# Attention scores of two pairs of heads in one go, with turns for the third PSUM pool

## The chip, the cores and the metric

The kernel runs on one core of a Trainium2 chip. The metric is the device time of one execution in microseconds (us). Before the change three timed runs gave 740.46, 740.71 and 740.96 us, with a median of 740.71. TensorE multiplies matrices into PSUM, VectorE (DVE) and ScalarE (ACT) do elementwise work, SyncE (SP) issues the loads. Each engine works through its own instructions in order.

## The reference

Two layers of a decoder trunk on 256 tokens of width 1024, in float32. The first half of a layer projects x once to the q, k and v of two attention branches of 8 heads of 64 each, and to two gates:

```python
def hybrid_mixer(x, w_in, w_branch_sb, w_branch_moba, w_out):
    S = x.shape[1]
    proj = x @ w_in
...
    o_sb = stick_breaking_attention(heads(q_sb, SB_HEADS), heads(k_sb, SB_HEADS), heads(v_sb, SB_HEADS))
    o_mb = moba_attention(partial_rope(heads(q_mb, MOBA_HEADS), pos),
                          partial_rope(heads(k_mb, MOBA_HEADS), pos),
                          heads(v_mb, MOBA_HEADS))
    branch_sb = merge_heads(o_sb) @ w_branch_sb
    branch_mb = merge_heads(o_mb) @ w_branch_moba
    merged = jax.nn.sigmoid(g_sb) * branch_sb + jax.nn.sigmoid(g_mb) * branch_mb
    return merged @ w_out
```

The stick-breaking weights of a query are sigmoid(z) times the product of sigmoid(-z) over all later keys before the query. The MoBA branch is, with 256 tokens and blocks of 256, a causal softmax. After the mixer come a normalised residual, a gated feed-forward of width 2816, and a second normalised residual.

## The kernel before

**Products.** Every float32 operand is split in two: `hi` holds its value rounded for TensorE's faster float32 mode, `lo` what is left. A product is then three matmuls, hi with hi, hi with lo and lo with hi. ScalarE makes hi (the cast at L48), VectorE makes lo (the subtraction at L53). The helper lines L48, L53 and L344 (`mm`) stand for most of the work, so the profile is read by tile names.

**Weights.** The weights come in 122 granules a layer of 128 x 1024 floats (512 KB) in the order in which they are used. `WeightStream` loads each to one of NRAW raw buffers, ScalarE and VectorE split it into one of ten places of the rings `whi` and `wlo`, and the raw buffer is free again. A projection to feature rows (`feat_major`: q and k of a stick-breaking pair, gates) uses a granule in 24 matmuls of 256 columns, one to token rows (`both_tokens`: v, and q and k of MoBA) in 12 of 512 columns.

**Attention.** Heads go in pairs: two heads of 64 rows lie in the 128 rows of a tile. The scores of a pair (`scores`, L460) are 12 matmuls on 64 rows each, two at a time, one for either head: three products for the first 128 queries against 128 keys, and three for the others against 256. VectorE adds the mask. In a stick-breaking pair (`sb_line`) ScalarE then computes two sigmoids, `keep` and `beta`, VectorE scans `keep` to `inc` and multiplies it into `beta`. In a MoBA pair (`mb_line`) VectorE takes maxima, ScalarE exponentials with their sums, VectorE scales. Then, for both (`weighted`): six transposes (L357) to `pT`, a split, six matmuls with v to `o`, and another split to the branch's output.

**Order.** The order of all instructions is written out when the program is built. The projections are the main line. Everything else is a generator, a "side", that yields the time at which its next step may be put in. The class `Weave` keeps an estimated time `t` of TensorE and of the other engines from the costs of what has been issued, and `tick`, called after every three matmuls, steps the sides that are due. The estimates set the order alone; the chip waits by semaphores.

**PSUM.** Three pools of two buffers each: `psM` for the projections (one bank a buffer), `psC` for the transposes of q, k, x and the feed-forward, and for `o` (one bank), `psB` for scores and `pT` (two banks). In layer order the stick-breaking pairs 0 to 3 are projected between the k and v of MoBA and the first gate; the MoBA pairs follow while gates 1 to 7 are projected, one every MB_GAP of estimated time.

Of the kernel before, what the change touches and what calls it, by code (L numbers as in the profile page):

```python
# [7 lines left out]
F32 = mybir.dt.float32  # L8
# [6 lines left out]
P = 128  # L15
# [19 lines left out]
class Weave:  # L35
# [31 lines left out]
    def _step(self, side):  # L67
        self.busy = True
        try:
            side[1] = next(side[0])  # L70
        except StopIteration:
            self.sides.remove(side)
        self.busy = False

    def tick(self):
# [104 lines left out]
ORDER = {2 * i + j: 4 * j + i for i in range(4) for j in range(2)}  # L180
NRAW = 6
NSPLIT = 10
# [15 lines left out]
def hybrid_trunk_kernel(ctx: ExitStack, tc: tile.TileContext, w, xT_in, x_in, ln_in,  # L198
# [32 lines left out]
    def bankB(name, shape):  # L231
        return psB.tile(shape, F32, tag="B", name=name)

    weave = Weave()
    rings = [p.tile([P, NSPLIT * GCOLS + on], F32R, name=n)
             for p, n, on in ((ring0, "whi", ON[0]), (ring1, "wlo", ON[1]))]
# [11 lines left out]
    xT_lo = big.tile([P, KC, S], F32R, name="xT_lo")  # L248
    mask = page2.tile([P, 2, P], F32, name="mask")
    warm = small.tile([P, 1], F32, tag="nmu", name="warm")  # L250
# [47 lines left out]
    nc.scalar.activation(warm, zero, AF.Sigmoid)  # L298
    busy = bankC("busy", [P, 512])
    for i in range(N_WARM):  # L300
        nc.tensor.matmul(busy, idle[:, :P], idle, start=True, stop=True)
# [61 lines left out]
    def pe_done():  # L363
        return weave.t + HOP
# [63 lines left out]
    def rope_line(name, ps, t, put):  # L428

        tmp = work.tile([P, 8, DH], F32, tag="T", name=f"{name}_tok{t}")  # L430
# [3 lines left out]
        a, b = (p.tile([P, n], F32, tag=tag, name=f"{name}_{tag}{t}")[:, :8 * ROPE]  # L434
                .rearrange("p (h r) -> p h r", h=8) for p, tag, n in ((page1, "ra", 240), (page2, "rb", 208)))
# [15 lines left out]
        yield from put(tp, slice(t * P, (t + 1) * P), pe_done())  # L451

    def scores(s, q, k, m):

        for c0, qs, ks in ((0, slice(0, P), slice(0, P)), (P, slice(P, S), slice(0, S))):
            for a, b in ((0, 0), (0, 1), (1, 0)):
                for h, rows in enumerate(ROWS):
                    nc.tensor.matmul(s[:, h, c0:c0 + ks.stop], q[a][rows, qs], k[b][rows, ks],  # L460
                                     start=a == b, stop=a == 1)
                weave.t += 0.11
        e = pe_done()
        yield e
        diag = s.rearrange("p h (a c) -> p h a c", c=256)[:, :, :, :P]
        e = dve(e, 512, nc.vector.tensor_add, diag, diag,
                mask[:, m, None, None, :].to_broadcast([P, 2, 2, P]))
        yield e
        return e

    def weighted(name, p, wt, v, oT, e):

        yield e + MARGIN
        pT = bankB(f"{name}_pT", [P, 2, 512])
        p_hi = page0.tile([P, 2, 384], F32R, tag="ph", name=f"{name}_ph")
        p_lo = page1.tile([P, 2, 384], F32R, tag="pl", name=f"{name}_pl")
        pe_after(e)
# [4 lines left out]
        e = pe_done()  # L482
        yield e
        e = yield from split_line(p_hi, p_lo, pT[:, :, :384], 768, e)
        yield e + MARGIN
        o = bankC(f"{name}_o", [P, 2, S])
        vs = slice(p * P, (p + 1) * P)
        pe_after(e)
        for part, a, b, first, last in ((o, 0, slice(0, S), True, False),
# [3 lines left out]
            mm(part, v[0][:, a, vs], p_lo[:, :, b], False, last)  # L493
        e = pe_done()
        yield e
        for h, hs in enumerate(ROWS):
            e = act(e, S, nc.scalar.copy, oT[0][hs, p, :], o[hs, h, :])
        yield e
        for h, hs in enumerate(ROWS):
            dve(e, S, nc.vector.tensor_sub, oT[1][hs, p, :], o[hs, h, :], oT[0][hs, p, :].bitcast(F32))  # L500

    BLOCKS = [(h, i, a, b) for h in range(2) for i, (a, b) in enumerate(((0, P), (P, 384)))]

    def sb_line(name, p, ps, hi, lo, v, oT, done):
        e = yield from split_line(hi, lo, ps, 512, pe_done())
        yield e + MARGIN
        s = bankB(f"{name}_s", [P, 2, 512])
        pe_after(e)
        e = yield from scores(s, *(((hi[:, i, :], lo[:, i, :])) for i in range(2)), 0)
        keep = work.tile([P, 2, 384], F32, tag="T", name=f"{name}_keep")  # L510
        beta = work.tile([P, 2, 384], F32, tag="T", name=f"{name}_beta")
        e1 = act(e, 768, nc.scalar.activation, keep, s[:, :, :384], AF.Sigmoid, scale=-0.125)
        e2 = act(e, 768, nc.scalar.activation, beta, s[:, :, :384], AF.Sigmoid, scale=0.125)
        done.append(name)
        yield e1
        inc = work.tile([P, 2, 384], F32, tag="T", name=f"{name}_inc")
# [3 lines left out]
        e = dve(e2, 768, nc.vector.tensor_mul, beta[:, :, :383], beta[:, :, :383], inc[:, :, 1:])  # L520
        yield from weighted(name, p, beta, v, oT, e)

    def mb_line(name, p, q, k, v, oT, before, done):
        while len(before) < NPAIR:
            yield weave.t + 0.1
        yield weave.t + MB_GAP * p
        s = bankB(f"{name}_s", [P, 2, 512])
        e = yield from scores(s, q, k, 1)
        nmax = small.tile([P, 2, 2], F32, tag="nmax", name=f"{name}_nmax")
# [16 lines left out]
        yield from weighted(name, p, ex, v, oT, e)  # L546

    halves = [slice(h * 512, (h + 1) * 512) for h in range(2)]
# [15 lines left out]
    def norm_line(name, t, junk, gb):  # L564
# [14 lines left out]
        for h in range(2):  # L579
            yield ends[h] + MARGIN  # L580
            tp = bankC(f"{name}_tp{t}{h}", [P, 4, P])
# [6 lines left out]
            yield e  # L588
            xT_ready[t] = yield from split_line(xT_hi[:, ks, ts], xT_lo[:, ks, ts], tp, 512, e)

# [32 lines left out]
    for l in range(DEPTH):  # L623
# [37 lines left out]
        sides, sigmoids, exps, gates, waiting = [], [], [], [], []  # L661

        def sb_pair(p, g):
# [5 lines left out]
            sides.append(weave.start(sb_line(f"{L}sb{p}", p, ps, hi, lo, v_sb, o_sb, sigmoids)))  # L669

# [12 lines left out]

        sb_pair(0, G + 8)
        k_mb = pair_tiles(L + "kmb", [P, NPAIR, S])
# [12 lines left out]
        o_mb = pair_tiles(L + "omb", [P, NPAIR, S])  # L698
        for p in range(NPAIR):
            q, k = ([part[:, p, :] for part in t] for t in (q_mb, k_mb))  # L700
            sides.append(weave.add(mb_line(f"{L}mb{p}", p, q, k, v_mb, o_mb, sigmoids, exps)))
        for c in range(1, KC):
# [44 lines left out]
        def h_line(name, ps, j, t):  # L747
# [4 lines left out]
            e = dve(e, 256, nc.vector.tensor_mul, sg, sg, ps[:, 256:])  # L752
            yield e + MARGIN
            tp = bankC(name + "T", [P, 2, P])
# [5 lines left out]
            yield e  # L760
            yield from split_line(h_t[0][0][:, 2 * j:2 * j + 2, ts], h_t[0][1][:, 2 * j:2 * j + 2, ts], tp, 256, e)

# [138 lines left out]
```

## Time and profile before

| | us |
|---|---|
| median of three timed runs | 740.71 |
| the profiled execution | 740.71 |
| its span, from the first to the last instruction | 738.9 |
| TensorE busy | 729.4 |
| VectorE busy | 515.7 |
| ScalarE busy | 387.9 |

The profile is of one execution. In names of tiles `l0` and `l1` are the layers; `pqk`, `pk`, `pu`, `pg` and `pb` the projections of a stick-breaking q and k, MoBA's k, MoBA's v, a gate and the branches; `sb` and `mb` the two kinds of pair. Buffer numbers are left out, so four pairs share a name. Matmuls are pipelined: a row's duration is longer than the distance to the next row's start. A row with x2 or x6 holds that many instructions.

### The profile page before, as it was taken

The page shows a single profiled execution, that of the slowest core. Times are in us where ns is not written, and L with a number is a line of the kernel's source. Part 1 is how long each engine was busy: PE and PEld are TensorE (multiplying, and loading weights), DVE is VectorE, ACT ScalarE, POOL GpSimd, SP SyncE. Part 2 cuts the span into 40 slices and gives each one's busy share as a digit, 9 for nine tenths or more (in the row PEclk, how much of TensorE's full clock was granted, in tenths as well). Part 3 has the DMA queues.
Part 4 walks back from the last instruction along what each step waited for, and adds up shares of the span by engine and source line. Part 5 has one row for each costly group of instructions (what it writes and reads, how often), then busy time and mean ns, then how long its engine had stood idle before and what let it go on. Part 6 is the DMA issues. An engine that isn't in the chain of part 4 may idle for free.

```text
span 738.9 us, 12698 instructions
## 1 busy us (share of the span) xinstructions
PE 729.4 (99%) x5112; PEld 669.3 (91%) x5112; DVE 515.7 (70%) x742; ACT 387.9 (52%) x575; POOL 13.4 (2%) x20
## 2 busy tenths in 40 slices
PE   9999999999999999999999999999999999999996
PEld 7888999998799999988888899999987999999885
DVE  5998876696886676643687787667878866665416
ACT  5765665863565455532375565566546655544300
POOL 0000000000000000000000000000010000000001
PEclk9999999999999999999999999999999999999998
DMA  8867622474486555465256364126646855553501
GB/s 303 335 211 246 227 81 92 170 243 150 178 274 216 197 199 193 179 259 195 74 198 241 143 200 144 58 86 228 232 167 201 281 191 194 190 200 129 214 1 57
DMA packets 39994, 136.32 MB, mean 184 GB/s; under 512 B 4480, under 2 KB 6528, under 8 KB 39936
## 3 DMA queue, kind: packets, MB, share of 16 engines
q1 hardware_dynamic: 39792, 135.25, 52.2%
q8 instruction: 40, 0.66, 0.3%
q10 hardware_dynamic: 144, 0.26, 0.1%
q14 instruction: 18, 0.15, 0.1%
HBM read 134.45 MB, written 1.05 MB: 183 GB/s over the span
## 4 chain that ended last, share of the span: by engine, by line
PE 94%; DVE 3%; issue 1%; ACT 1%; POOL 1%; POOLq 0%; DVEq 0%; ACTq 0%
PE l1pf L344 13%; PE l0pf L344 13%; PE l0pd L344 8%; PE l0pg L344 6%; PE l1pg L344 6%; PE l1pe L344 4%; PE l1pd L344 4%; PE l0pqk L344 3%; PE l1pvq L344 3%; PE l1pb L344 3%; PE l0pb L344 3%; PE l1pqk L344 3%; PE l0pw L344 2%; PE l1pw L344 2%; PE l1pft L344 2%; PE l0pft L344 2%
## 5 line engine op out<-in xcount | busy, mean ns | idle before, releaser
L53 DVE TENSOR_TENSOR wlo<-raw,whi 128x1024 fp32r<-128x1024 f32 (+1 forms) x248 | 296.3, 1206 | 84.2 <-ACT whi L48 81.0
L48 ACT CAST whi<-raw 128x1024 fp32r<-128x1024 f32 (+1 forms) x247 | 253.6, 1037 | 84.8 <-PE l0pd L344 20.8
L344 PE MATMUL l1pf<-xT_hi,whi 128*128 128x256 f32 x288 | 79.7, 277 | 0.0
L344 PE MATMUL l1pf<-xT_hi,wlo 128*128 128x256 f32 x288 | 79.6, 276 | 0.0
L344 PE MATMUL l1pf<-xT_lo,whi 128*128 128x256 f32 x288 | 79.6, 276 | 0.0
L344 PE MATMUL l0pf<-xT_hi,whi 128*128 128x256 f32 x288 | 79.6, 276 | 0.0
L344 PE MATMUL l0pf<-xT_hi,wlo 128*128 128x256 f32 x288 | 79.5, 276 | 0.0
L344 PE MATMUL l0pf<-xT_lo,whi 128*128 128x256 f32 x288 | 79.5, 276 | 0.0
L344 PEld LDWEIGHTS l1pf<-xT_lo,whi 128*128 128x128 f32 x288 | 54.1, 188 | 0.0
L344 PEld LDWEIGHTS l1pf<-xT_hi,whi 128*128 128x128 f32 x288 | 54.1, 188 | 0.0
L344 PEld LDWEIGHTS l1pf<-xT_hi,wlo 128*128 128x128 f32 x288 | 54.1, 188 | 0.0
L344 PEld LDWEIGHTS l0pf<-xT_lo,whi 128*128 128x128 f32 x288 | 54.1, 188 | 0.0
L344 PEld LDWEIGHTS l0pf<-xT_hi,whi 128*128 128x128 f32 x288 | 54.1, 188 | 0.0
L344 PEld LDWEIGHTS l0pf<-xT_hi,wlo 128*128 128x128 f32 x288 | 54.1, 188 | 0.0
L344 PE MATMUL l1pg<-xT_hi,whi 128*128 128x256 f32 x128 | 36.6, 286 | 0.0
L344 PE MATMUL l0pg<-xT_hi,whi 128*128 128x256 f32 x128 | 36.6, 286 | 0.0
L344 PE MATMUL l1pg<-xT_hi,wlo 128*128 128x256 f32 x128 | 35.6, 278 | 0.0
L344 PE MATMUL l0pg<-xT_hi,wlo 128*128 128x256 f32 x128 | 35.6, 278 | 0.0
L344 PE MATMUL l1pg<-xT_lo,whi 128*128 128x256 f32 x128 | 35.5, 277 | 0.0
L344 PE MATMUL l0pg<-xT_lo,whi 128*128 128x256 f32 x128 | 35.5, 277 | 0.0
L344 PE MATMUL l0pd<-whi,l0h_hi 128*128 128x512 f32 x88 | 34.4, 391 | 0.0
L344 PE MATMUL l0pd<-whi,l0h_lo 128*128 128x512 f32 x88 | 34.3, 389 | 0.0
(382 smaller groups left out, 1764.0 us busy)
## 6 DMA issues: line engine op xcount, KB each, us to landing
raw<-in_w_dram SPq DMA_DIRECT2D x240, 512.0 KB, 4.1
ln<-in_ln_dram SPq DMA_DIRECT2D x8, 512.0 KB, 6.2
raw<-in_w_dram SPq DMA_DIRECT2D x7, 256.0 KB, 5.1
x<-in_x_dram SPq DMA_DIRECT2D x2, 512.0 KB, 6.7
out_dram<-x SPq DMA_DIRECT2D x3, 256.0 KB, 2.0
xT_raw<-in_xT_dram SPq DMA_DIRECT2D x4, 128.0 KB, 4.0
xT_raw<-in_xT_dram SPq DMA_DIRECT2D x2, 256.0 KB, 6.4
raw<-in_w_dram ACTq DMA_DIRECT2D x1, 256.0 KB, 2.8
```

The costliest lines, as they stand in the source:

```text
L48: f(*args, **kw)
L53: f(*args, **kw)
L344: nc.tensor.matmul(o, a, b, start=start, stop=stop)
```

## The change

The q and k of two stick-breaking pairs are projected next to each other (pairs 0 and 1, then MoBA's k and v, then pairs 2 and 3, then gate 0), and the granules are renumbered to match. `two_pairs` takes both buffers of `psB`, issues the scores of both pairs, 24 matmuls, and starts a side for each. The MoBA pairs go by two in the same way. `weighted` uses one tile `pp` for both split weights of all pairs; lists (`begun`, `turned`, `summed`, `passed`) keep the sides in an order in which a buffer is asked for after its last reader has been issued. The odd stick-breaking pair's `keep` gets a tile of its own, and its `beta` waits for the even pair's product. A step that takes a buffer of `psC` asks `turn` for the estimated time at which the buffer two turns earlier is left. Sides may yield nothing, which means "look again soon", and `finish` steps the next side that can go on. To make room there are five raw buffers in place of six; the rope's copies go to the pool of 4 KB units, and the mask to another page.

```diff
     def finish(self, sides):
-        left = [s for s in sides if s in self.sides]
-        while left:
-            side = min(left, key=lambda s: s[1])
-            self._step(side)
-            left = [s for s in left if s in self.sides]
+        while left := [s for s in sides if s in self.sides]:
+            for side in sorted(left, key=lambda s: s[1]):
+                if not self._step(side):
+                    break
...
 ORDER = {2 * i + j: 4 * j + i for i in range(4) for j in range(2)}
-NRAW = 6
+
+for _g in (0, NG_LAYER):
...
+        ORDER[_g + _i] = _g + _j
+NRAW = 5
...
+    def turn(e):
+
+        was = None
+        while True:
+            k = taken[0] - 2
+            if k >= 0 and k not in left:
+                yield
+            elif (e := max(e, left.get(k, 0.0))) == was:
+                break
+            else:
+                was = e
+                yield e + MARGIN
+        taken[0] += 1
+        return taken[0] - 1
...
+    def scores(pairs):
+
+
+        for s, q, k in pairs:
+            for c0, qs, ks in ((0, slice(0, P), slice(0, P)), (P, slice(P, S), slice(0, S))):
+                for a, b in ((0, 0), (0, 1), (1, 0)):
+                    for h, rows in enumerate(ROWS):
+                        nc.tensor.matmul(s[:, h, c0:c0 + ks.stop], q[a][rows, qs], k[b][rows, ks],
+                                         start=a == b, stop=a == 1)
+                    weave.t += 0.11
+        return pe_done()
...
-        p_hi = page0.tile([P, 2, 384], F32R, tag="ph", name=f"{name}_ph")
-        p_lo = page1.tile([P, 2, 384], F32R, tag="pl", name=f"{name}_pl")
+        begun.append(name)
+        mine = len(begun)
+        p_hi, p_lo = (pp[:, i] for i in range(2))
...
+        while len(summed) < mine:
+            yield
+        e = max(e, summed[-1])
+        yield e
         e = yield from split_line(p_hi, p_lo, pT[:, :, :384], 768, e)
-        yield e + MARGIN
+        turned.append(e)
+        i = yield from turn(e)
         o = bankC(f"{name}_o", [P, 2, S])
...
+    def two_pairs(line, name, ps, qks, free, e, sides, *args):
+
+
+        while len(turned) < free:
+            yield
+        e = max(e, *turned[max(free - 2, 0):free], 0.0)
+        yield e + MARGIN
+        ss = [bankB(f"{name}{p}_s", [P, 2, 512]) for p in ps]
+        pe_after(e)
+        e = scores([(s, *qk) for s, qk in zip(ss, qks)])
+        for p, s in zip(ps, ss):
+            sides.append(weave.add(line(f"{name}{p}", p, s, e, *args)))
...
-        both_tokens(f"{L}pk", G + 10, lambda t, ps: ropes.append(weave.start(rope_line(L + "kmb", ps, t, put_kmb))))
-        sb_pair(1, G + 14)
+        both_tokens(f"{L}pk", G + 12, lambda t, ps: ropes.append(weave.start(rope_line(L + "kmb", ps, t, put_kmb))))
...
         sb_pair(2, G + 20)
-        gate(0, G + 22)
-        sb_pair(3, G + 24)
+        sb_pair(3, G + 22)
+        gate(0, G + 24)
```

What this does to the order is shown at three places. A number behind a name is the buffer's in the program.

TensorE, in layer 0 at the scores of the third stick-breaking pair, before:

```order
L344 MATMUL l0pg_816<-xT_hi,wlo 128x256
L460 MATMUL l0sb_s<-l0qkhi_739 128x128 x2
L460 MATMUL l0sb_s<-l0qklo_740,l0qkhi_739 128x128 x2
L460 MATMUL l0sb_s<-l0qkhi_739,l0qklo_740 128x128 x2
L460 MATMUL l0sb_s<-l0qkhi_739 128x256 x2
L460 MATMUL l0sb_s<-l0qklo_740,l0qkhi_739 128x256 x2
L460 MATMUL l0sb_s<-l0qkhi_739,l0qklo_740 128x256 x2
L344 MATMUL l0pg_816<-xT_hi,whi 128x256
```

and now, where the fourth pair's stand right behind them (a gate product follows):

```order
L484 MATMUL l0sb_s<-l0qkhi_741 128x128 x2
L484 MATMUL l0sb_s<-l0qklo_742,l0qkhi_741 128x128 x2
L484 MATMUL l0sb_s<-l0qkhi_741,l0qklo_742 128x128 x2
L484 MATMUL l0sb_s<-l0qkhi_741 128x256 x2
L484 MATMUL l0sb_s<-l0qklo_742,l0qkhi_741 128x256 x2
L484 MATMUL l0sb_s<-l0qkhi_741,l0qklo_742 128x256 x2
L484 MATMUL l0sb_s<-l0qkhi_810 128x128 x2
L484 MATMUL l0sb_s<-l0qklo_811,l0qkhi_810 128x128 x2
L484 MATMUL l0sb_s<-l0qkhi_810,l0qklo_811 128x128 x2
L484 MATMUL l0sb_s<-l0qkhi_810 128x256 x2
L484 MATMUL l0sb_s<-l0qklo_811,l0qkhi_810 128x256 x2
L484 MATMUL l0sb_s<-l0qkhi_810,l0qklo_811 128x256 x2
```

The score products of a pair are the same twelve; in place of two visits between ordinary products there is one.

VectorE at the same pair, from the split of its q and k to its product, before (`wlo` is the lo part of a weight granule):

```order
L53 TENSOR_TENSOR l0qklo_740<-l0pqk_741,l0qkhi_739 128x512
L53 TENSOR_TENSOR wlo<-raw_666,whi 128x1024
L53 TENSOR_TENSOR wlo<-raw_705,whi 128x1024
L53 TENSOR_TENSOR l0sb_s<-l0sb_s,mask 128x4x128
L53 TENSOR_TENSOR wlo<-raw_728,whi 128x1024
L53 SCALAR_TENSOR_TENSOR l0sb_inc<-l0sb_keep,zero 128x128
L53 SCALAR_TENSOR_TENSOR l0sb_inc<-l0sb_keep,zero 128x256
L53 SCALAR_TENSOR_TENSOR l0sb_inc<-l0sb_keep,zero 128x128
L53 SCALAR_TENSOR_TENSOR l0sb_inc<-l0sb_keep,zero 128x256
L53 TENSOR_TENSOR l0sb_beta<-l0sb_beta,l0sb_inc 128x2x383
```

and now, from the last weight split ahead of both masks to the second pair's product:

```order
L53 TENSOR_TENSOR wlo<-raw_791,whi 128x1024
L53 TENSOR_TENSOR l0sb_s<-l0sb_s,mask 128x4x128 x2
L53 SCALAR_TENSOR_TENSOR l0sb_inc<-l0sb_keep,zero 128x128
L53 SCALAR_TENSOR_TENSOR l0sb_inc<-l0sb_keep,zero 128x256
L53 SCALAR_TENSOR_TENSOR l0sb_inc<-l0sb_keep,zero 128x128
L53 SCALAR_TENSOR_TENSOR l0sb_inc<-l0sb_keep,zero 128x256
L53 TENSOR_TENSOR l0sb_beta<-l0sb_beta,l0sb_inc 128x2x383
L53 SCALAR_TENSOR_TENSOR l0sb_inc<-l0sb_keep,zero 128x128
L53 SCALAR_TENSOR_TENSOR l0sb_inc<-l0sb_keep,zero 128x256
L53 SCALAR_TENSOR_TENSOR l0sb_inc<-l0sb_keep,zero 128x128
L53 SCALAR_TENSOR_TENSOR l0sb_inc<-l0sb_keep,zero 128x256
L53 TENSOR_TENSOR l0sb_beta<-l0sb_beta,l0sb_inc 128x2x383
```

Both masks stand ahead of the first pair's scans, and no weight split stands between the two pairs' work.

ScalarE at the end of layer 0's attention, from the cast of the last pair's transposes to its output, before:

```order
L48 CAST l0mb_ph<-l0mb_pT 128x768
L48 CAST whi<-raw_1168 128x1024
L48 ACT_TABLE_LOAD
L48 ACTIVATE l0gate_1474<-l0pg_1475 128x512
L48 CAST whi<-raw_1232 128x1024
L48 CAST l0omb_hi<-l0mb_o 64x256 x2
```

and now, from the third pair's transposes to the fourth pair's output:

```order
L48 CAST pp<-l0mb_pT 128x768
L48 ACT_TABLE_LOAD
L48 ACTIVATE l0gate_1452<-l0pg_1453 128x512
L48 CAST whi<-raw_1291 128x1024
L48 CAST whi<-raw_1305 128x1024
L48 CAST l0omb_hi<-l0mb_o 64x256 x2
L48 CAST pp<-l0mb_pT 128x768
L48 CAST whi<-raw_1344 128x1024
L48 ACTIVATE l0gate_1452<-l0pg_1528 128x512
L48 CAST l0omb_hi<-l0mb_o 64x256 x2
```

The last pair's cast stands behind the third pair's two output casts, since `pp` is one tile.

## Rows read from the trace of the kernel before

**Rows 1.** The page: its head, the busy time of the engines, and the shares of the engines in the chain of work that ended last.

```profile
span 738.9 us, 12698 instructions
...
PE 729.4 (99%) x5112; PEld 669.3 (91%) x5112; DVE 515.7 (70%) x742; ACT 387.9 (52%) x575; POOL 13.4 (2%) x20
...
PE 94%; DVE 3%; issue 1%; ACT 1%; POOL 1%; POOLq 0%; DVEq 0%; ACTq 0%
```

**Rows 2.** The list of waits, of TensorE alone: who waited for whom, us in total, times, longest us.

```profile
PE busy L301 <- DVE mhalf L297: 1.5, 1, 1.5
PE l1a_tp L357 <- DVE xT_lo L53: 0.4, 1, 0.4
PE l0a_tp L357 <- DVE xT_lo L53: 0.3, 1, 0.3
```

**Rows 3.** The timeline of TensorE around the scores of the third pair in layer 0, between gate products of 256 columns: start us, us, engine, line, operation, output and operands, rows and columns of the stationary side, moving operand, count.

```profile
75.34 0.28 PE L344 MATMUL l0pg<-xT_hi,whi 128*128 128x256 f32 x1
...
75.90 0.28 PE L344 MATMUL l0pg<-xT_hi,wlo 128*128 128x256 f32 x1
76.11 0.33 PE L460 MATMUL l0sb_s<-l0qkhi 64*128 64x128 f32 x2
...
76.79 0.28 PE L460 MATMUL l0sb_s<-l0qkhi,l0qklo 64*128 64x256 f32 x2
77.00 0.38 PE L344 MATMUL l0pg<-xT_hi,whi 128*128 128x256 f32 x1
77.22 0.28 PE L344 MATMUL l0pg<-xT_lo,whi 128*128 128x256 f32 x1
```

**Rows 4.** The same view around the scores of the first pair in layer 0, between k products of 512 columns.

```profile
37.44 0.39 PE L344 MATMUL l0pk<-whi,xT_hi 128*128 128x512 f32 x1
...
37.90 0.39 PE L344 MATMUL l0pk<-whi,xT_lo 128*128 128x512 f32 x1
38.22 0.33 PE L460 MATMUL l0sb_s<-l0qkhi 64*128 64x128 f32 x2
...
38.89 0.28 PE L460 MATMUL l0sb_s<-l0qkhi,l0qklo 64*128 64x256 f32 x2
...
39.45 0.39 PE L344 MATMUL l0pk<-wlo,xT_hi 128*128 128x512 f32 x1
```

**Rows 5.** The same view, the first gate product behind the first MoBA scores of layer 0.

```profile
92.64 0.38 PE L344 MATMUL l0pg<-xT_hi,whi 128*128 128x256 f32 x1
```

**Rows 6.** The instructions of the line that issues the scores, by tile: engine, operation, count, duration in ns (least, median, most), first and last start in us, forms. The first of four tiles that read alike.

```profile
L460 PE MATMUL l0sb_s<-l0qkhi x16: 322/328/331, 38.2 to 89.3; 64*128 64x128 f32 x8, 64*128 64x256 f32 x8
```

**Rows 7.** The timeline of VectorE behind those first scores: mask, scans, product.

```profile
39.22 0.70 DVE L53 TENSOR_TENSOR l0sb_s<-l0sb_s,mask 128x512 f32<-128x512 f32 x1 [0.45 <-PE l0sb_s L460]
...
40.95 1.90 DVE L53 TENSOR_TENSOR_SCAN l0sb_inc<-l0sb_keep,zero 128x128 f32<-128x128 f32 x4
42.96 0.96 DVE L53 TENSOR_TENSOR l0sb_beta<-l0sb_beta,l0sb_inc 128x766 f32<-128x766 f32 x1
```

**Rows 8.** The chain that ended last, in order of time: start us, us, what. A visit to output products and one to transposes in layer 0.

```profile
87.22 1.05 PE l0sb_o L344 x6
...
113.69 0.66 PE l0mb_pT L357 x6
```

**Rows 9.** The timelines of ScalarE and of VectorE around the first MoBA exponentials of layer 0: table load, first exponential, the reading of the last sum, the scaling.

```profile
98.29 1.28 ACT L48 ACT_TABLE_LOAD   x1
99.59 0.37 ACT L48 ACTIVATE l0mb_e<-l0mb_s,l0mb_nmax 128x128 f32<-128x128 f32 x1
...
101.09 0.21 ACT L48 ACTIVATION_READ_ACCUMULATOR l0mb_e<-l0mb_s,l0mb_nmax 128x1 f32 x1
...
101.55 1.01 DVE L53 TENSOR_SCALAR l0mb_e<-l0mb_e,l0mb_rec 128x128 f32<-128x128 f32 x4
```

**Rows 10.** Groups of instructions by line and shape on ScalarE and on VectorE, 30 to 140 us (attention of layer 0): busy us, mean ns of one, and behind the bar the idle time before them.

```profile
L48 ACT CAST whi<-raw 128x1024 fp32r<-128x1024 f32 x34 | 35.1, 1052 | 2.5 <-issue 1.3 <-PE l0pqk L344 1.1
...
L48 ACT COPY l0gate<-l0pg 128x512 f32<-128x512 f32 x6 | 3.5, 588 | 6.4 <-PE l0pg L344 6.3
...
L48 ACT CAST l0mb_ph<-l0mb_pT 128x768 fp32r<-128x768 f32 x4 | 3.2, 804 | 7.8 <-PE l0mb_pT L357 7.8
...
L48 ACT CAST l0osb_hi<-l0sb_o 64x256 fp32r<-64x256 f32 x8 | 3.0, 369 | 2.8 <-PE l0sb_o L344 2.7
...
L53 DVE TENSOR_TENSOR wlo<-raw,whi 128x1024 fp32r<-128x1024 f32 x33 | 39.9, 1223 | 5.4 <-ACT whi L48 5.0 <-PE l0qmb_tp L357 0.2
...
L53 DVE TENSOR_TENSOR l0mb_pl<-l0mb_pT,l0mb_ph 128x768 fp32r<-128x768 f32 x4 | 3.8, 954 | 1.9 <-ACT l0mb_ph L48 1.9
L53 DVE TENSOR_TENSOR l0osb_lo<-l0sb_o,l0osb_hi 64x256 fp32r<-64x256 f32 x8 | 3.4, 420 | 0.9 <-ACT l0osb_hi L48 0.9
```

**Rows 11.** The timelines of TensorE and of ScalarE in layer 1, around the transposes of the third pair; in brackets the idle time of the engine just before, and what ended it.

```profile
445.52 0.28 PE L344 MATMUL l1pqk<-xT_hi,wlo 128*128 128x256 f32 x1
445.85 0.88 PE L357 MATMUL l1sb_pT<-ident,l1sb_beta 128*128 128x128 f32 x6
...
440.61 1.05 ACT L48 CAST whi<-raw 128x1024 fp32r<-128x1024 f32 x1 [2.21 <-issue]
```

**Rows 12.** The page's DMA issues (KB of one, median us from issue to landing), and from the list of waits what ScalarE waited for a weight to land.

```profile
raw<-in_w_dram SPq DMA_DIRECT2D x240, 512.0 KB, 4.1
...
ACT whi L48 <- DMA raw<-in_w_dram: 7.4, 9, 1.8
```

More of the change, by code (lines that the diff above doesn't have):

```diff
@@ L67, in _step @@
     def _step(self, side):
-        self.busy = True
+        self.busy, e = True, 0.0
         try:
-            side[1] = next(side[0])
+            e = next(side[0])
+            side[1] = self.t + 0.1 if e is None else e
         except StopIteration:
@@ L180 @@
 ORDER = {2 * i + j: 4 * j + i for i in range(4) for j in range(2)}
-NRAW = 6
+for _g in (0, NG_LAYER):
+    for _i, _j in ((10, 14), (11, 15), (12, 10), (13, 11), (14, 12), (15, 13),
+                   (22, 24), (23, 25), (24, 22), (25, 23)):
+        ORDER[_g + _i] = _g + _j
+NRAW = 5
 NSPLIT = 10
@@ L234, in hybrid_trunk_kernel @@
     weave = Weave()
+    taken, left = [0], {}
+    def turn(e):
[11 more added lines that the diff above has]
+        return taken[0] - 1
     rings = [p.tile([P, NSPLIT * GCOLS + on], F32R, name=n)
@@ L248, in hybrid_trunk_kernel @@
     xT_lo = big.tile([P, KC, S], F32R, name="xT_lo")
-    mask = page2.tile([P, 2, P], F32, name="mask")
+    mask = page1.tile([P, 2, P], F32, name="mask")
     warm = small.tile([P, 1], F32, tag="nmu", name="warm")
@@ L299, in hybrid_trunk_kernel @@
     busy = bankC("busy", [P, 512])
+    taken[0], left[0] = 1, 0.0
     for i in range(N_WARM):
@@ L428, in rope_line @@
     def rope_line(name, ps, t, put):
-        tmp = work.tile([P, 8, DH], F32, tag="T", name=f"{name}_tok{t}")
+        tmp = unit(f"{name}_tok{t}", [P, 8, DH])
         e = act(pe_done(), WIDTH, nc.scalar.copy, tmp, ps.rearrange("p (h d) -> p h d", d=DH))
@@ L434, in rope_line @@
         a, b = (p.tile([P, n], F32, tag=tag, name=f"{name}_{tag}{t}")[:, :8 * ROPE]
-                .rearrange("p (h r) -> p h r", h=8) for p, tag, n in ((page1, "ra", 240), (page2, "rb", 208)))
+                .rearrange("p (h r) -> p h r", h=8) for p, tag, n in ((page1, "ra", 240), (page2, "rb", 464)))
         cc = rope[:, t, 0, None, :].to_broadcast([P, 8, ROPE])
@@ L450, in rope_line, with masked @@
         yield pe_done()
[L451 to L464, printed above, removed]
+        left[i] = yield from put(tp, slice(t * P, (t + 1) * P), pe_done())
+    def scores(pairs):
[7 more added lines that the diff above has]
+        return pe_done()
+    def masked(s, m, e):
         diag = s.rearrange("p h (a c) -> p h a c", c=256)[:, :, :, :P]
[L466 to L469, printed above, removed]
+        return dve(e, 512, nc.vector.tensor_add, diag, diag,
+                   mask[:, m, None, None, :].to_broadcast([P, 2, 2, P]))
+    begun, turned, summed = [], [], [0.0]
+    pp = page1.tile([P, 2, 2, 384], F32R, name="pp")
     def weighted(name, p, wt, v, oT, e):
@@ L483, in weighted @@
         yield e
+        while len(summed) < mine:
+            yield
+        e = max(e, summed[-1])
+        yield e
         e = yield from split_line(p_hi, p_lo, pT[:, :, :384], 768, e)
-        yield e + MARGIN
+        turned.append(e)
+        i = yield from turn(e)
         o = bankC(f"{name}_o", [P, 2, S])
@@ L494, in weighted @@
         e = pe_done()
+        summed.append(e)
         yield e
@@ L499, in weighted, with sb_line @@
         for h, hs in enumerate(ROWS):
-            dve(e, S, nc.vector.tensor_sub, oT[1][hs, p, :], o[hs, h, :], oT[0][hs, p, :].bitcast(F32))
+            left[i] = dve(e, S, nc.vector.tensor_sub, oT[1][hs, p, :], o[hs, h, :], oT[0][hs, p, :].bitcast(F32))
     BLOCKS = [(h, i, a, b) for h in range(2) for i, (a, b) in enumerate(((0, P), (P, 384)))]
[L504 to L511, printed above, removed]
+    def sb_line(name, p, s, e, v, oT, done, passed):
+        yield e
+        e = masked(s, 0, e)
+        yield e
+        keep = (page0 if p % 2 else work).tile([P, 2, 384], F32, tag="T", name=f"{name}_keep")
+        if p % 2 == 0:
+            inc, beta = (work.tile([P, 2, 384], F32, tag="T", name=f"{name}_{n}") for n in ("inc", "beta"))
         e1 = act(e, 768, nc.scalar.activation, keep, s[:, :, :384], AF.Sigmoid, scale=-0.125)
+        if p % 2:
+            while len(passed) < p:
+                yield
+            inc, beta = (work.tile([P, 2, 384], F32, tag="T", name=f"{name}_{n}") for n in ("inc", "beta"))
         e2 = act(e, 768, nc.scalar.activation, beta, s[:, :, :384], AF.Sigmoid, scale=0.125)
@@ L520, in sb_line, with mb_line @@
         e = dve(e2, 768, nc.vector.tensor_mul, beta[:, :, :383], beta[:, :, :383], inc[:, :, 1:])
+        passed.append(name)
         yield from weighted(name, p, beta, v, oT, e)
[L523 to L528, printed above, removed]
+    def mb_line(name, p, s, e, v, oT, done):
+        yield e
+        e = masked(s, 1, e)
+        yield e
         nmax = small.tile([P, 2, 2], F32, tag="nmax", name=f"{name}_nmax")
@@ L579, in norm_line @@
         for h in range(2):
-            yield ends[h] + MARGIN
+            i = yield from turn(ends[h])
             tp = bankC(f"{name}_tp{t}{h}", [P, 4, P])
@@ L588, in norm_line @@
             yield e
-            xT_ready[t] = yield from split_line(xT_hi[:, ks, ts], xT_lo[:, ks, ts], tp, 512, e)
+            left[i] = xT_ready[t] = yield from split_line(xT_hi[:, ks, ts], xT_lo[:, ks, ts], tp, 512, e)
     xT_ready = [0.0, 0.0]
@@ L661, in hybrid_trunk_kernel @@
         sides, sigmoids, exps, gates, waiting = [], [], [], [], []
+        passed, ends, qks = [], {}, {}
         def sb_pair(p, g):
@@ L668, in sb_pair, with line @@
             feat_major(ps[:, 1, :], g + 1)
-            sides.append(weave.start(sb_line(f"{L}sb{p}", p, ps, hi, lo, v_sb, o_sb, sigmoids)))
+            qks[p] = [(hi[:, i, :], lo[:, i, :]) for i in range(2)]
+            def line():
+                ends[p] = yield from split_line(hi, lo, ps, 512, pe_done())
+                if p % 2:
+                    e = max(ends[p - 1], ends[p])
+                    yield e + MARGIN
+                    yield from two_pairs(sb_line, f"{L}sb", (p - 1, p), (qks[p - 1], qks[p]),
+                                         l * 2 * NPAIR + p - 1, e, sides, v_sb, o_sb, sigmoids, passed)
+            sides.append(weave.start(line()))
         def gate(c, g):
@@ L694, in hybrid_trunk_kernel, with mb_two @@
         sb_pair(2, G + 20)
-        gate(0, G + 22)
-        sb_pair(3, G + 24)
+        sb_pair(3, G + 22)
+        gate(0, G + 24)
         weave.finish(ropes)
         o_mb = pair_tiles(L + "omb", [P, NPAIR, S])
-        for p in range(NPAIR):
-            q, k = ([part[:, p, :] for part in t] for t in (q_mb, k_mb))
-            sides.append(weave.add(mb_line(f"{L}mb{p}", p, q, k, v_mb, o_mb, sigmoids, exps)))
+        def mb_two(p):
+            while len(sigmoids) < NPAIR:
+                yield
+            yield weave.t + MB_GAP * p
+            yield from two_pairs(mb_line, f"{L}mb", (p, p + 1),
+                                 [[[part[:, i, :] for part in t] for t in (q_mb, k_mb)] for i in (p, p + 1)],
+                                 l * 2 * NPAIR + NPAIR + p, 0.0, sides, v_mb, o_mb, exps)
+        for p in (0, 2):
+            sides.append(weave.add(mb_two(p)))
         for c in range(1, KC):
@@ L752, in h_line @@
             e = dve(e, 256, nc.vector.tensor_mul, sg, sg, ps[:, 256:])
-            yield e + MARGIN
+            k = yield from turn(e)
             tp = bankC(name + "T", [P, 2, P])
@@ L760, in h_line @@
             yield e
-            yield from split_line(h_t[0][0][:, 2 * j:2 * j + 2, ts], h_t[0][1][:, 2 * j:2 * j + 2, ts], tp, 256, e)
+            left[k] = yield from split_line(h_t[0][0][:, 2 * j:2 * j + 2, ts], h_t[0][1][:, 2 * j:2 * j + 2, ts],
+                                            tp, 256, e)
         def swiglu_line(name, ps, hi, lo):
```

4 lines of the change are left out of this document (3 added, 1 removed).

## The prediction

> **What bounds the kernel now.** I read the page first: TensorE is busy for 729.4 of 738.9 us, and the chain of work that ended last is 94% TensorE [rows 1]. Then the list of what TensorE waited for: three waits, 2.2 us in all, 1.5 of them before the first matmul [rows 2]. So nothing that another engine does faster can help by much. Time is won only where TensorE itself passes its products slowly, and lost only where the new order makes it wait. The profiled execution took 740.71 us, its span 738.9, and 740.71 is also the median of the three timed runs; I add to and subtract from that number.
>
> Where does TensorE pass slowly? A product's duration in the trace overlaps the next one's, so I read start to start. In an undisturbed stretch the 256-column products stand 0.11 us apart (75.34 to 75.90: five steps, 0.56 us) [rows 3] and the 512-column ones 0.23 (37.44 to 37.90: two steps, 0.46) [rows 4]. Around the scores, products on half the rows of the array that run two at a time, it is otherwise. From the last ordinary product before them to the second after them are 75.90 to 77.22, 1.32 us. Two ordinary steps are 0.23 of that. The scores are six steps: five from 76.11 to 76.79, and one more of 0.11, so 0.79. What is left, 0.30 us, is the price of going to the scores and back: 0.10 before the first of them, 0.10 after the last, and 0.10 to 0.11 behind the first ordinary product, which shows as 0.38 long instead of 0.28 [rows 3]. Between 512-column products the same sum is 1.55 - 0.46 - 0.78 = 0.31 [rows 4]. MoBA scores, whose q and k were ready many microseconds before, have the same long ordinary product behind them, so the loss is not a wait for an operand [rows 5].
>
> **The change, part by part.**
>
> *Scores of two pairs in one go.* The trace has 16 products of each kind of score for each branch and layer: four pairs, two heads, two halves, and four such tiles [rows 6]. That makes 16 visits of 12 products. In the new order the score products are as many and stand in 8 visits of 24; the visits to transposes number 43 in either order. So 8 x 0.30 = 2.4 us go. Bounds: the scores' own opening step is 0.16 instead of 0.11 (0.68 for five steps [rows 3] holds two such); if one of them belongs to entering, 0.35 go per visit, 2.8 us; if the 0.10 before the first score has another reason and stays, 0.20 go, 1.6 us. I take 2.4: the second half of a pair opens as slowly, with no change of shape before it.
>
> *New hand-overs.* What TensorE does while VectorE and ScalarE prepare its next step is fixed by the order; I set the one against the other. Stick-breaking, one pair, before: the last score begins at 38.89 and ends by 39.2, the mask begins at 39.22 [rows 4, 7], then come sigmoids and scans, and the product ends at 43.92: 4.75 us. After, the second pair's mask (0.70) stands behind the first's on VectorE, beside the first's sigmoid, which hides it; the second pair's scans and product come 1.90 + 0.11 + 0.96 = 2.97 later, at 7.7. Between the scores and the first pair's transposes the new order has 30 products of 512 columns in layer 0 (6.8 us), 24 in layer 1 (5.45), and for pairs 2 and 3 of either layer 48 of 256 (5.45): 0.7 us to spare at the tightest three places. Up to the second pair's transposes come six transposes (0.66 us [rows 8]) and 2.4 to 2.7 us of products: 8.5 or more against 7.7. The new wait on ScalarE, the odd pair's second sigmoid for the even pair's product, whose scan tile it overwrites, ends about 4.8 us after the scores. Behind it in that queue stand a k or gate copy and the cast of the first transposes, which TensorE releases only later: it holds up nothing.
>
> MoBA: the exponentials of a pair take 1.7 (99.59 to 101.30), the scaling until 102.56 another 1.26, the table load 1.28 [rows 9]. In front of the load stands a gate copy, 0.59 [rows 10], of a gate that is 18 products or 2.0 us away; masks and reductions of the first pair end earlier. First pair: 2.0 + 0.6 + 1.3 + 1.7 + 1.3 = 6.9, against 72 products of 256, 8.2 us. Second: 6.9 + 1.7 = 8.6, against 8.2 + 0.7 + 1.8 = 10.7.
>
> A pair's two split weights now lie in one tile for all pairs, as one buffer of each did before; the second pair's casts wait for the first pair's output products. Behind these come two output casts 0.74, cast 0.80, subtraction 0.96 and some 0.15 between them, 2.7 us [rows 10], with two or three weight splits queued in between. The order leaves 33 products (3.75 us), at the end of the attention 30 (3.4). There I walk it through, from the end of the third pair's MoBA transposes at 0. ScalarE: cast to 0.85, table load 2.15, gate 2.7, two weight casts 4.75, output casts 5.5, pair cast 6.3. VectorE: weights 4.95 and 6.1, output subtractions 6.95, pair 7.9. TensorE is there at 0.1 + 2.4 + 0.7 + 0.4 + 1.05 + 3.4 = 8.0, and nothing is left to cover more than that. The branch projection behind it needs this output 21 products (2.4 us) later. I put 0.1 us for each layer here and 0.1 for the rest together: +0.3. Bounds 0 and 2 us (half of 40 hand-overs, 16 transposes, 16 outputs and 8 scores, late by 0.1).
>
> *A stall that goes.* The product at 445.52 is followed by transposes only 0.33 later, 0.22 too late: ScalarE had sat idle for 2.21 us before the weight cast at 440.61, and VectorE followed it [rows 11]. These transposes get 5.45 us of cover: -0.2, between 0 and -0.22. The waits before the norm's transposes [rows 2] keep their cover and stay.
>
> *The output products* read the split weights from another tile. A visit takes 1.05 us [rows 8], against 3 x 0.227 + 3 x 0.113 = 1.02 at ordinary pace. So between 0 and 16 x 0.03 = 0.5; I take -0.2.
>
> *One raw weight buffer fewer.* A buffer is held from issue to landing, 4.1 us [rows 12], then for 1.05 and 1.22 of splitting [rows 10], say 6.6 with gaps: five buffers allow a granule each 1.3 us, and TensorE uses one in 24 x 0.113 = 2.7. Counted in the new order, VectorE's splits stand at least 5.5 granules ahead of TensorE at every hand-over, where before 4.8 was the least. Cost 0, at most one wait like the longest of ScalarE for a weight, 1.8 us [rows 12]; the nearest of these rows cost TensorE nothing.
>
> *Turns in the third pool* only choose places in the order, which is counted above. Every engine and queue, SP's too, issues as many instructions as before; ten granules a layer are loaded at other places of the same stream. The rope's copies take slots of another pool, the mask another page: nothing counted.
>
> Sum: -2.4 + 0.3 - 0.2 - 0.2 = -2.5, so 738.2 us.
>
> **The rivals.**
>
> Half eaten. The savings come, but hand-overs are late by 0.1 us at 14 more of the 40 places: 739.6. For it: the two-pair clumps hold VectorE for some 7 us on end, and it is the busiest engine beside TensorE, 70% [rows 1]. Against it: the covers above.
>
> Slower. ScalarE, which works in order, is held by a weight cast as for 2.21 us at 440.61 [rows 11], in front of the first sigmoid at the three places with 0.7 us to spare and in front of the last pair's cast in each layer. It would cost 1.5 us at each of the three and 2.1 at the two: 8.7 less the 2.8 of gain, 746.6. It is slower from 0.9 us of lateness at each of the five on. Against it: in the new order the weight casts before these sigmoids fill places of the ring that TensorE left nearly a granule, 2.4 us, or more before.
>
> The visit is not what costs. If the loss hung on each pair's group of products and not on the change of shape, half of it would stay inside the visit: 739.4. Against it: between a pair's two halves nothing like 0.3 is lost.
>
> The banks. Before, the scores of a pair and the transposes of its neighbour share the two large PSUM buffers in turn. After, both go to scores at once, and the second MoBA visit waits until both pairs' transposes are read. That is covered by 3.75 against 2.7 us plus what is queued between; with two weight splits of 1.15 in full, 1.2 us are lost at each of two visits: 740.6. Against it: the splits stand early in that queue and run beside the second transposes and the output. The Trainium skill ("Perfetto Trace Analysis", section Matmuls) says that independent groups should rotate through different banks, so that the evacuation of one overlaps the matmuls of the next; that speaks against taking both at once, and for this rival. In this trace products of another pool lie under every evacuation, so the rule is met without the two buffers.
>
> **How the numbers follow.** Forecast 738.2 with 0.74; half eaten 0.11; the visit 0.05; the banks 0.04; slower 0.06. A measurement of this kernel can tell about 0.2%, 1.5 us, so faster begins below 739.2. The forecast lies there, the three middle rivals within 0.2%, with a little of the first on the faster side: faster 0.75, same 0.19, slower 0.06. Range: below, -2.8 - 0.2 - 0.5 + 0 is 737.2; above, "half eaten" and "the visit" with some more lateness, 740.0.
>
> **What would show it.** Eight score visits of 24 products, 1.6 us each, with one 0.38 product behind each where columns are 256; TensorE's waits still three lines; transposes and outputs with ordinary steps before them, except perhaps the last output of each layer. It is wrong if the second pair's scores open with 0.3 us of their own, if transposes of stick-breaking weights start 0.3 or more late, or if TensorE waits for a weight split anywhere in the attention.

## The result, and the profile after

The changed kernel takes 736.04 us (median of six runs, 735.88 to 736.94) against 740.77 of the kernel before (six runs too). The ratio is 0.9938 with a 95% interval of 0.9925 to 0.995, so 4.7 us less (3.7 to 5.6). The prediction had 2.5 less. The profiled spans, 734.4 and 738.9 us, are 4.5 apart.

The page of the changed kernel, the lines of [rows 1]:

```profile
span 734.4 us, 12694 instructions
...
PE 725.3 (99%) x5112; PEld 667.7 (91%) x5112; DVE 516.4 (70%) x742; ACT 387.6 (53%) x575; POOL 13.4 (2%) x20
...
PE 98%; DMA 1%; SPq 0%; DVE 0%; POOL 0%; POOLq 0%; ACT 0%; issue 0%; DVEq 0%
```

TensorE has the same 5112 matmuls and its share of the chain rose from 94% to 98%: less of the chain now runs through other engines. The list of TensorE's waits, the view of [rows 2], tells which part went:

```profile
PE busy L325 <- DVE mhalf L320: 1.5, 1, 1.5
PE l0pq L368 <- ACT whi L48: 0.3, 1, 0.3
```

Both waits before the norm's transposes are gone. The prediction had said that they stay. The new 0.3 us is a wait for one of the first weights, which ends at 9.63. Of the runs below with the same start, runs 1 and 2 have no such line and run 3 has one of 0.4, and all four come to the first q and k product of the stick-breaking pairs within 0.12 us (27.81 here; 27.76, 27.85 and 27.88), so I do not count it.

The timeline of TensorE in the changed kernel, five stretches: the first scores of layer 0 between 512-column products, as [rows 4]; the second ones between gate products, as [rows 3]; the last output of layer 0; the norm's second transposes; the third pair's transposes of layer 1, as [rows 11]. The columns are those of [rows 3].

```profile
42.50 0.39 PE L368 MATMUL l0pk<-whi,xT_lo 128*128 128x512 f32 x1
...
44.73 0.40 PE L368 MATMUL l0pk<-wlo,xT_hi 128*128 128x512 f32 x1
...
81.25 0.28 PE L368 MATMUL l0pg<-xT_hi,wlo 128*128 128x256 f32 x1
81.46 0.33 PE L484 MATMUL l0sb_s<-l0qkhi 64*128 64x128 f32 x2
81.62 0.28 PE L484 MATMUL l0sb_s<-l0qklo,l0qkhi 64*128 64x128 f32 x2
...
82.25 0.22 PE L484 MATMUL l0sb_s<-l0qkhi 64*128 64x128 f32 x2
82.31 0.28 PE L484 MATMUL l0sb_s<-l0qklo,l0qkhi 64*128 64x128 f32 x2
...
82.82 0.28 PE L484 MATMUL l0sb_s<-l0qkhi,l0qklo 64*128 64x256 f32 x2
83.03 0.38 PE L368 MATMUL l0pg<-xT_hi,whi 128*128 128x256 f32 x1
83.25 0.28 PE L368 MATMUL l0pg<-xT_lo,whi 128*128 128x256 f32 x1
...
137.42 0.39 PE L368 MATMUL l0mb_o<-pp,l0vmb_hi 128*128 128x512 f32 x1
137.65 0.39 PE L368 MATMUL l0mb_o<-pp,l0vmb_lo 128*128 128x512 f32 x1
137.88 0.51 PE L368 MATMUL l0mb_o<-pp,l0vmb_hi 128*128 128x512 f32 x2
...
193.08 0.39 PE L368 MATMUL l0pft<-whi,xT_lo 128*128 128x512 f32 x1
193.31 0.60 PE L381 MATMUL l0a_tp<-ident,x 128*128 128x128 f32 x4
193.66 0.47 PE L368 MATMUL l0pft<-whi,xT_hi 128*128 128x512 f32 x1
193.98 0.48 PE L368 MATMUL l0pft<-wlo,xT_hi 128*128 128x512 f32 x1
194.30 0.40 PE L368 MATMUL l0pft<-whi,xT_lo 128*128 128x512 f32 x1
...
449.31 0.28 PE L368 MATMUL l1pg<-xT_hi,wlo 128*128 128x256 f32 x1
449.43 0.82 PE L381 MATMUL l1sb_pT<-ident,l1sb_beta 128*128 128x128 f32 x6
```

*Scores.* From the last gate product before the scores to the second after them are 81.25 to 83.25, 2.00 us for two pairs. Before, one pair took 1.32 with two ordinary steps in it [rows 3]. Two such visits hold four ordinary steps and the double one two, so the two visits stand for 2 x 1.32 - 0.23 = 2.41, and a visit saved is worth 0.41 us. With 512-column neighbours it is 2 x 1.55 - 0.46 - (44.73 - 42.50) = 0.41 as well. Eight of them: 3.3 us. The prediction's 0.30 is the outside of a visit; the other 0.11 lies inside: the second pair's first product is followed 0.06 later (82.25 to 82.31), where a pair that opens a visit needs 0.16 (81.46 to 81.62).

*The norm.* From the last product before the second transposes to the third product after them are 193.08 to 194.30, 1.22 us. The same stretch of the kernel before:

```profile
193.23 0.40 PE L344 MATMUL l0pft<-whi,xT_lo 128*128 128x512 f32 x1
193.93 0.66 PE L357 MATMUL l0a_tp<-ident,x 128*128 128x128 f32 x4 [0.30 <-DVE xT_lo L53]
...
194.89 0.39 PE L344 MATMUL l0pft<-whi,xT_lo 128*128 128x512 f32 x1
```

It took 1.66, so 0.44 is gone here, and 0.50 in layer 1 by the same reading: 0.9 us. The bracket says 0.30, but the step from 193.23 to 193.93 is 0.70 where it is 0.23 in the changed kernel: the price of a wait is read from the starts, not from the idle time alone. The bank is one of `psC`, the third pool, and making `xT_lo` is the read that frees it. In the changed kernel's order 9 products of 512 columns stand between the feed-forward's transposes and these, before only 3: `turn` put the step where the estimate says that the bank is free.

*The stall* at 445.52 [rows 11] is gone: 449.31 to 449.43 is 0.12, where it was 0.33. Sum: 3.3 + 0.9 + 0.2 = 4.4 of the 4.5 us. That it closes so well is partly luck. At the first q and k product the changed kernel is 0.2 us behind (27.81 against 27.61). From there to the first branch product of its layer, the attention is shorter by 1.75 us in layer 0 and by 2.17 in layer 1, where the scores and the stall account for 1.6 and 1.9. The other 0.4 us have no cause here.

### The profile page after: what moved, and what is told of

The parts are those of the page before. It is cut to its first block, busy times and chain, and to the rows that moved or that the text cites. A ratio compares the mean times of both kernels' runs of the same rounds, so it can differ in the third digit from the quotient of the medians.

```text
span 734.4 us, 12694 instructions
## 1 busy us (share of the span) xinstructions
PE 725.3 (99%) x5112; PEld 667.7 (91%) x5112; DVE 516.4 (70%) x742; ACT 387.6 (53%) x575; POOL 13.4 (2%) x20
## 4 chain that ended last, share of the span: by engine, by line
PE 98%; DMA 1%; SPq 0%; DVE 0%; POOL 0%; POOLq 0%; ACT 0%; issue 0%; DVEq 0%
PE l1pf L368 13%; PE l0pf L368 13%; PE l0pd L368 8%; PE l1pg L368 6%; PE l0pg L368 6%; PE l1pe L368 4%; PE l1pd L368 4%; PE l1pqk L368 3%; PE l0pqk L368 3%; PE l1pft L368 3%; PE l0pft L368 3%; PE l0pw L368 3%; PE l1pvq L368 3%; PE l1pw L368 3%; PE l0pb L368 3%; PE l1pb L368 3%
```

## The experiments

**1. Do the second pair's cheap steps come from the other bank or from the change of columns?** The changed kernel with both pairs' first halves ahead of both second halves.

```diff
-        for s, q, k in pairs:
-            for c0, qs, ks in ((0, slice(0, P), slice(0, P)), (P, slice(P, S), slice(0, S))):
+        for c0, qs, ks in ((0, slice(0, P), slice(0, P)), (P, slice(P, S), slice(0, S))):
+            for s, q, k in pairs:
```

> The changed kernel, with the two pairs' scores taken in turn by halves: first the first 128 queries of either pair, then the others of either. In the changed kernel's trace a visit has four openings: 0.16 (first pair, first half), 0.17 (first pair, second half), 0.06 (second pair, first half), 0.17 (second pair, second half), where other steps are 0.11. Theory 'bank': an opening is slow where the group begins in the PSUM bank that was written just before it. Then only the entry stays at 0.16 and the three others are 0.06: 2 x 0.11 less per visit, 8 visits, 1.8 us, so 734.3. Theory 'columns': it is slow where the moving side goes from 128 to 256 columns. Then one of the four stays at 0.17: 0.11 less per visit, 0.9 us, so 735.2. If neither, 736.0.

Measured: 736.3 us, ratio to before 0.9941 (0.9928 to 0.9953), the changed kernel's own time. Neither theory's gain came. TensorE's timeline at the same scores:

```profile
81.39 0.33 PE L484 MATMUL l0sb_s<-l0qkhi 64*128 64x128 f32 x2
81.55 0.28 PE L484 MATMUL l0sb_s<-l0qklo,l0qkhi 64*128 64x128 f32 x2
...
81.78 0.28 PE L484 MATMUL l0sb_s<-l0qkhi 64*128 64x128 f32 x2
81.89 0.28 PE L484 MATMUL l0sb_s<-l0qklo,l0qkhi 64*128 64x128 f32 x2
...
82.11 0.33 PE L484 MATMUL l0sb_s<-l0qkhi 64*128 64x256 f32 x2
82.28 0.28 PE L484 MATMUL l0sb_s<-l0qklo,l0qkhi 64*128 64x256 f32 x2
...
82.52 0.28 PE L484 MATMUL l0sb_s<-l0qkhi 64*128 64x256 f32 x2
82.64 0.28 PE L484 MATMUL l0sb_s<-l0qklo,l0qkhi 64*128 64x256 f32 x2
82.75 0.28 PE L484 MATMUL l0sb_s<-l0qkhi,l0qklo 64*128 64x256 f32 x2
```

Where only the bank changes (81.78, 82.52) the step is an ordinary 0.11 to 0.12. Where columns go from 128 to 256 (82.11) it is 0.17, in this order once instead of twice; but the short step of 0.06, which in the changed kernel stands where columns go back from 256 to 128, is gone with it. From first to last score product are 1.36 us in either order (81.39 to 82.75; 81.46 to 82.82). So a change of bank alone alters nothing, and the step from 128 to 256 columns is 0.17 with a change of bank (here) and without one (inside each pair of the changed kernel). The step of 0.06 was seen only where bank and columns change together. Both theories on what would be won missed.

**2. Is it the going and returning that costs?** The changed kernel with two ordinary products between the two pairs' scores. They write to the second pair's bank, whose scores then overwrite them, so they only add work.

```diff
-        for s, q, k in pairs:
+        for n, (s, q, k) in enumerate(pairs):
+            if n:
+                for x in (xT_hi, xT_lo):
+                    nc.tensor.matmul(s[:, 0, :S], xT_hi[:, 0, :P], x[:, 0, :], start=True, stop=True)
```

> The changed kernel, with two ordinary products of 256 columns put between the two pairs' scores of each visit (into the second pair's bank, where the scores overwrite them; the result is unchanged). It doubles the visits to 16 again with all else in place, and so measures what a visit costs. The two products alone are 2 x 0.113 x 8 = 1.8 us. Theory 'a visit costs 0.41' (1.32 + 1.32 - 2.00 - 0.23 from the two traces): 8 x 0.41 = 3.3 more, 741.1. My prediction's 0.30: 2.4 more, 740.3. If the loss does not hang on the visit: 737.9.

Measured: 741.17 us, 5.1 above the changed kernel. The 16 added products are worth 16 x 0.112 = 1.8 at the pace of [rows 3]; what is left is 3.3, or 0.41 for each of eight visits, the number read from the timelines. TensorE's timeline:

```profile
82.78 0.28 PE L487 MATMUL l0sb_s<-l0qkhi,l0qklo 64*128 64x256 f32 x2
82.99 0.39 PE L483 MATMUL l0sb_s<-xT_hi 128*128 128x256 f32 x1
83.21 0.28 PE L483 MATMUL l0sb_s<-xT_lo,xT_hi 128*128 128x256 f32 x1
83.42 0.33 PE L487 MATMUL l0sb_s<-l0qkhi 64*128 64x128 f32 x2
83.59 0.27 PE L487 MATMUL l0sb_s<-l0qklo,l0qkhi 64*128 64x128 f32 x2
```

All parts are back: 0.21 into the ordinary products and 0.21 out of them instead of 0.11, 0.22 behind the first, and an opening step of 0.17 instead of 0.06. The rival "the visit is not what costs" falls with it. The Trainium skill ("TensorEngine Tiling (Array Packing)", section Key Properties) says that a change of tiling mode drains TensorE; the run is in keeping with that, with 0.10 us lost on entering and 0.10 on leaving. That it is a drain which takes them no run shows.

**3. Is it the turns that took the norm's waits away?** The changed kernel, with the norm's transposes put in as before, without asking `turn`; everything else of the change stays. TensorE's order then differs from the changed kernel's at the norm's second transposes, in both layers, and nowhere else.

```diff
-            i = yield from turn(ends[h])
+            yield ends[h] + MARGIN
+            taken[0] += 1
+            i = taken[0] - 1
```

> The changed kernel with the norm's transposes asking no turn for their bank of the third PSUM pool: they are due as before the change. Theory 'turns': the two waits of 0.47 and 0.54 us before the second token half's second transposes, which the changed kernel no longer has, come back, at the same place and for VectorE's reading of the bank: 737.0. Rival 'lighter queue': they went because VectorE reaches this stage with other work in its queue; then they stay away: 736.0.

Measured: 737.07 us (736.68 to 737.33), 1.0 above the changed kernel. Its list of TensorE's waits has, besides the two lines of the changed kernel's:

```profile
PE l1a_tp L381 <- DVE xT_lo L53: 0.4, 1, 0.4
PE l0a_tp L381 <- DVE xT_lo L53: 0.3, 1, 0.3
```

They are the lines of [rows 2] again. The two-pair scores and five raw buffers, which this kernel keeps, did not take them away.

**4. Does the same place in the order help the kernel before?** The kernel before, with the second transposes of each token tile asked for only after the first ones' split.

```diff
-            yield ends[h] + MARGIN
+            yield max(ends[h], xT_ready[t] if h else 0.0) + MARGIN
```

> The kernel before, with one edit: the second transposes of a norm are due only when the estimate has the first ones' split done. Theory 'turns': both waits go without anything else of the change, 1.0 us: 739.75, TensorE then waits only before its first matmul. Rival 'lighter queue': the waits stay or come elsewhere: 740.8.

Measured: 740.27 us, 0.5 less, ratio 0.9996 (0.9987 to 1.0005), which does not tell it from no change. It does not rule out the 0.9 either. The waits are gone from the list, and the traces show about half of the gain: from the start of the first q and k product of the stick-breaking pairs to that of TensorE's last product are 703.24 us, against 703.73 before (703.69 in run 6, which has the same order) and 702.86 in run 5 below. The timeline behind the moved transposes:

```profile
194.57 0.39 PE L344 MATMUL l0pft<-whi,xT_lo 128*128 128x512 f32 x1
194.81 0.60 PE L357 MATMUL l0a_tp<-ident,x 128*128 128x128 f32 x4
195.16 0.48 PE L344 MATMUL l0pft<-whi,xT_hi 128*128 128x512 f32 x1
195.54 0.50 PE L344 MATMUL l0pft<-wlo,xT_hi 128*128 128x512 f32 x1
195.88 0.40 PE L344 MATMUL l0pft<-whi,xT_lo 128*128 128x512 f32 x1
```

The stretch takes 1.31 us here against 1.22 in the changed kernel, with steps of 0.38 and 0.34 in place of 0.32 and 0.32. This edit also moves other transposes, of the norms, the feed-forward and MoBA's q, so it was no clean test of the turns; why the steps are longer stays open.

**5. The turns alone.** The kernel before with `turn` at every taker of the third pool and the `Weave` that it needs, pairs one by one, six raw buffers. TensorE's order then differs from that of before at three places alone: the norm's second transposes in both layers, and one of MoBA's k transposes in layer 1.

```diff
-            yield ends[h] + MARGIN
+            i = yield from turn(ends[h])
...
-            xT_ready[t] = yield from split_line(xT_hi[:, ks, ts], xT_lo[:, ks, ts], tp, 512, e)
+            left[i] = xT_ready[t] = yield from split_line(xT_hi[:, ks, ts], xT_lo[:, ks, ts], tp, 512, e)
```

> The kernel before with the turns alone (turn() asked by every taker of the third pool, and the Weave that it needs), pairs still one by one, six raw buffers. TensorE's order moves at three places: the second transposes of the norm stand 6 products of 512 columns later in both layers, MoBA's k transposes of layer 1 stand 12 products later; nothing on SP. Theory 'turns': the waits of 0.3 and 0.4 us before l0a_tp and l1a_tp go from the list, and all of the 0.9 to 1.0 us that taking the turns away from the changed kernel cost comes here too: 739.8 (span 737.9). Rival 'given back': as in the run that only asked for the norm's transposes later, half of it is lost again behind the moved transposes: 740.2. Rival 'nothing', which the prediction had taken: 740.7, with the waits still in the list or as long elsewhere.

Measured: 739.86 us (median of 11), ratio 0.999 (0.9982 to 0.9999): 0.9 less. Of TensorE's waits only the first remains:

```profile
PE busy L320 <- DVE mhalf L315: 1.5, 1, 1.5
```

And its timeline has the stretch at 194.91 to 196.13, 1.22 us as in the changed kernel:

```profile
194.91 0.39 PE L363 MATMUL l0pft<-whi,xT_lo 128*128 128x512 f32 x1
...
196.13 0.40 PE L363 MATMUL l0pft<-whi,xT_lo 128*128 128x512 f32 x1
```

Put in alone the turns win 0.9 us (0.1 to 1.3 by the interval, and 0.9 by the traces, 703.73 - 702.86); taken away alone they cost 1.0. What run 3 has left, 3.7 below the kernel before, is what the scores and the stall come to, 3.3 + 0.2, within 0.2.

**6. One raw buffer fewer.** The kernel before with five in place of six; the order is the same on every engine.

```diff
-NRAW = 6
+NRAW = 5
```

> The kernel before with five raw weight buffers in place of six and nothing else; the order of the instructions is the same on every engine. Theory (the prediction's term, 0): 740.7, and TensorE's waits are the same three lines. Rival 'loads late': one wait of TensorE for a weight like the longest of ScalarE for a landing weight, 1.8 us: 742.5. Rival 'smoother loads': fewer weights in flight leave the first loads sooner, and the start gets shorter by up to 0.5: 740.2.

Measured: 740.99 us, ratio 1.0002 (0.9993 to 1.0011): no cost that can be told. But the list of ScalarE's waits has, for the line of [rows 12],

```profile
ACT whi L48 <- DMA raw<-in_w_dram: 16.9, 15, 4.9
```

where six buffers gave 7.4, and 1.8 for the longest; the changed kernel has 17.6 and 4.7. The two longest, 4.9 and 4.6 us, end before TensorE comes to the weight. At the start one reaches TensorE, whose list has, besides the three lines of [rows 2],

```profile
PE l0pv L344 <- ACT whi L48: 0.2, 1, 0.2
```

So the rival "loads late" came in small, 0.2 us where it had 1.8. Such a wait for one of the first weights is listed in three of the five traces with five buffers (this one, the changed kernel, run 3) and in none of the three with six. The first q and k product of the stick-breaking pairs begins at 27.49 to 27.91 with six buffers and at 27.76 to 27.95 with five: a cost of 0.1 or 0.2 us cannot be told from this spread, and is not ruled out.

## Why the prediction was wrong

The direction held: TensorE stayed the bound, and what was won was won where it passed its products slowly or waited. The time fell below the range because two steps were wrong on the same side.

*Scores of two pairs in one go*, -2.4, measured -3.3. The term was mis-sized, and so was its bound of 2.8. The step that failed is "I take 2.4: the second half of a pair opens as slowly, with no change of shape before it". It is true of the second half, whose columns go from 128 to 256. A second pair opens after 256 columns with 128, which the trace of before did not hold anywhere, and there the step is 0.06 instead of 0.16: cheaper than an ordinary step, where the bound had allowed for no less than ordinary. A visit of 24 products takes 1.36 + 0.11 = 1.47 us, where the prediction had 1.6. Run 1's order saves the same 0.11 inside a visit in another way: it opens once (0.16) and goes from 128 to 256 columns once (0.17), where two pairs one by one do each twice.

*Turns in the third pool* "only choose places in the order, which is counted above", and "the waits before the norm's transposes [rows 2] keep their cover and stay": a term put at nothing, measured -0.9, shown from both sides by runs 3 and 5. The places in the attention were counted; the 6 products more in front of the norm's second transposes were not, though the two lines of [rows 2] were the only waits of TensorE that could go. Their price would have been short too: the list says 0.7, the time says 0.9.

*New hand-overs*, +0.3, measured 0: none is in the list of waits. The place that I walked through, the last pair of a layer, came as worked out: from the end of the third pair's transposes (129.64) VectorE's split of the last pair ends at 7.88 (forecast 7.9) and TensorE is there at 7.78 (8.0). VectorE's timeline:

```profile
136.56 0.96 DVE L53 TENSOR_TENSOR pp<-l0mb_pT,pp 128x768 fp32r<-128x768 f32 x1
```

It ends at 137.52, after the output products begin at 137.42, and still nothing waits: the first two of them read the cast half, and the first to read VectorE's half comes third, at 137.88. The 0.1 that I put here had a reserve of 0.4 (137.52 to 137.88) which I had not looked up.

*A stall that goes*, -0.2: measured -0.21. *The output products*, -0.2: measured 0. The chain of waits shows a visit in the changed kernel at the same length as in [rows 8]:

```profile
56.77 1.05 PE l0sb_o L368 x6
```

Reading the weights from another tile does not matter. This miss and that of the hand-overs nearly cancel, by luck. *One raw weight buffer fewer*, 0: no cost that can be told (run 6), though ScalarE's wait of 1.8 that I had taken for the longest possible grew to 4.9, and 0.2 us of waiting reached TensorE at the start. The rivals that end slower did not show: no first sigmoid or last cast held TensorE up, and the second MoBA visits, where "the banks" would wait, are entered in 0.2 us like the others:

```profile
116.69 0.28 PE L368 MATMUL l0pg<-xT_hi,wlo 128*128 128x256 f32 x1
116.89 0.33 PE L484 MATMUL l0mb_s<-l0kmb_hi,l0qmb_hi 64*128 64x128 f32 x2
```

## What to carry to other kernels

A visit to matmuls of another shape has a price outside and inside; take it from a timeline that holds the sequence to come, or bound it without assuming that a step can be no shorter than an ordinary one. When a change touches how places in the order are chosen, go through the list of waits line by line and look up in the new order what stands in front of each, also far from the code that the change is about. Before a late operand is priced, look which of the consumer's first instructions reads it.

## What the hardware showed that I had not expected

Among products on half the rows the distance to the next one follows the columns before and after: 0.11 us between equal ones, 0.17 where 128 columns are followed by 256, 0.06 where 256 are followed by 128 (82.25 in the changed kernel). A change of bank alone leaves it at 0.11; the 0.06 was seen only together with one. The long and the short step make two ordinary ones, 0.23, so putting equal columns together won nothing (run 1). And five raw buffers in place of six more than doubled ScalarE's waits for landing weights, 7.4 to 16.9 us, with no time that can be told (run 6).
